# The second FFN pass of a hybrid attention/mLSTM step: its down products as scaled float16 pairs, in groups of 6, 6, 6 and 4 tiles

## The chip, the cores and the metric

The program runs on one core of one Trainium2 chip, in one launch. The metric is the device time of an execution in microseconds (us), compared by the median of several runs. One execution was also recorded by the hardware profiler; all traces and profile lines are of such an execution.

Engines are written as in the profile: PE is TensorE's matmuls, PEld its weight loads, DVE is VectorE, ACT is ScalarE, POOL is GpSimd, SP is SyncE, whose queue issues most loads.

## The reference

One step of a hybrid diffusion backbone in float32: 128 prompt tokens and 1024 latent tokens, model width 1024, one layer. Attention and a bidirectional mLSTM memory stand side by side, then one output projection, then a SwiGLU FFN of width 2816. Only the FFN and what is behind it matter here:

```python
def swiglu(h, w_gu, w_down):
    g, u = jnp.split(h @ w_gu, 2, axis=-1)
    return (jax.nn.silu(g) * u) @ w_down
...
    h2 = rmsnorm(x, norm2_w) * (1 + sc2) + sh2
    x = x + g2 * swiglu(h2, w_gu, w_down)
...
y = rmsnorm(x, final_norm_w)
```

`w_gu` is 1024 x 5632, `w_down` is 2816 x 1024. The 1152 tokens are 9 blocks of 128.

## The kernel before

**Tiling.** The width of the FFN is cut into 22 tiles (NF) of 128. The FFN runs twice over all weights. A first pass does blocks 0 to 2 (the prompt and two latent blocks). The second pass does the other 6 blocks (768 tokens), and the change is in it.

**Precision by pairs.** A value is split into a high part and a remainder ("hi" and "lo"), and a product of two such values is three matmuls: hi·hi, hi·lo and lo·hi. The gate and up products of the second pass use pairs of float16, scaled by powers of two that are found at run time: `six` holds those scales, and `wsum` row sums from which a bound on the weights is made (`tally` in `load_piece`, then `weight_scale` and `power_scale`). The down products use pairs of float32r instead, without a scale.

**The second pass, tile by tile.** `pair6` makes one tile f of the FFN's width for all 768 tokens, in a scheme of 7 products instead of 8 (Strassen's kind). Each product is 12 matmuls of 128x128 by 128x384, so a tile, called a pair from here on, is 84 matmuls. `weights6` loads the two weight halves (512 KB each) and makes the operands `A` of the products: four sums `S` on VectorE, then scaled high halves on ScalarE and low halves on VectorE. Between products, ScalarE copies the first product (`p1`) and takes two Tanh (`tn`), and VectorE does the other sums. At a pair's end `hl` holds the activation of tile f: high half by ScalarE (L1663), low half by VectorE (L1664).

**Down products.** After a group of tiles (`SIX`: 4, 4, 4, 4, 3, 3), `down6` loads that group's rows of `w_down`, two tiles of 512 columns to a piece (512 KB). For each half n of the width and each of 6 blocks, `down_block6` adds three matmuls of 128x128 by 128x512 per tile into one PSUM bank; `hl` is the stationary operand. That is 22 x 12 x 3 = 792 matmuls. `add_gated` (L1205 and L1206, on VectorE) then multiplies the bank by the gate `gs6` and adds it to the tokens' rows: 12 times per group, 72 times in all. The last group goes through `down_last`, which also does the final RMSNorm of a block and writes it out.

**What sets the order.** The program is written once and a scheduler with a simulated timeline orders each engine's instructions; so the down products of a group end up among and behind products of the next pair. Tiles have tags with a fixed number of buffers. There are four raw buffers for weights that come in as float32, and four pieces, each a high and a low half, under four tags of two buffers. A piece is used again in turn. Eight PSUM banks serve the whole pass. SyncE's queue issues loads in its order.

Of the kernel before, what the change touches and what calls it, by code (L numbers as in the profile page):

```python
# [8 lines left out]
F32 = mybir.dt.float32  # L9
F32R = mybir.dt.float32r  # L10
F16 = mybir.dt.float16
# [38 lines left out]
def hybrid_step(ctx: ExitStack, tc: tile.TileContext, I: dict, O: dict):  # L50
# [24 lines left out]
    def emit(gen):  # L75
        for _ in gen:
            pass
# [79 lines left out]
    def load_piece(srcs, shape, raw=None, own=None, tally=None):  # L157

        a, b = shape
        n = a * b  # L160

        def view(t):
            return t[:, :n].rearrange("p (a b) -> p a b", b=b)

        raw = raw_tile() if raw is None else raw
        if not own:
            loaded["n"] = (loaded["n"] + 1) % len(piece_tags)
            tag = piece_tags[loaded["n"]]
# [5 lines left out]
        nc.scalar.copy(hi[:, :n], raw[:, :n])  # L174
        sub(lo[:, :n], raw[:, :n], hi[:, :n].bitcast(F32), "dve")
        if tally is not None:
            jk = ft.tile([P, D], BF16, name=nm("jk"), tag="t2", bufs=nt2[0])
            act(jk[:, :n], hi[:, :n].bitcast(F32), AF.Abs, accum_out=wsum[:, tally : tally + 1])
        return view(hi), view(lo)

    full_view = lambda v: v
# [13 lines left out]
    def power_scale(tp, one, bound, out):  # L195
# [4 lines left out]
        dve.tensor_reduce(out=v[:, 0:1], in_=ps[0:1, 0:P], axis=AX.X, op=ALU.max)  # L200
        powers(v, 1)
# [1326 lines left out]
    def six_scales():  # L1528

        dve.tensor_reduce(out=six[:, 6:7], in_=shift2[:, :, 1], axis=AX.X, op=ALU.max, apply_absolute_value=True)  # L1530
        dve.tensor_reduce(out=six[:, 7:8], in_=scale2[:, :, 1], axis=AX.X, op=ALU.max, apply_absolute_value=True)
        dve.scalar_tensor_tensor(out=six[:, 7:8], in0=six[:, 7:8], scalar=float(D) ** 0.5, in1=six[:, 6:7], op0=ALU.mult, op1=ALU.add)
        yield
        yield from power_scale(fp, ones, six[:, 7:8], six[:, 0:2])
        for t, src in ((0, scale2), (1, shift2)):
            dve.tensor_scalar(out=mods6[:, :, t], in0=src[:, :, 1], scalar1=six[:, 0:1], scalar2=None, op0=ALU.mult)
        yield

    def weight_scale():

        dve.tensor_reduce(out=six[:, 7:8], in_=wsum, axis=AX.X, op=ALU.max)
        emit(power_scale(fp, ones, six[:, 7:8], six[:, 2:4]))
# [71 lines left out]
    def pair6(f, Bt, acts):  # L1614
# [45 lines left out]
        dve.tensor_tensor(out=tn[:, 0], in0=tn[:, 0], in1=a, op=ALU.mult)  # L1660
        hl = new_hl(f)
        flat = tn.rearrange("p a n -> p (a n)")
        act(hl[:, 0], flat, AF.Copy, scale=six[:, 6:7])  # L1663
        dve.scalar_tensor_tensor(out=hl[:, 1], in0=flat, scalar=six[:, 6:7], in1=hl[:, 0].bitcast(F32), op0=ALU.mult, op1=ALU.subtract)  # L1664
        acts.append(hl)
        yield

    late_hl = {}

    def new_hl(f):  # L1670
        if f % 6 < 4:
            return up.tile([P, 2, 2 * CT], F32R, name=nm("hl"), tag="hl", bufs=4)
        if "t" not in late_hl:
            late_hl["t"] = rowp.tile([P, 2, 2, 2 * CT], F32R, name="hl_late", tag="b4")
        return late_hl["t"][:, f % 6 - 4]

    def down_pieces6(f0, nf, n):
        pieces = []
        for j in range(0, nf, 2):
            m = min(2, nf - j)  # L1680
            rows = w_down[(f0 + j) * P : (f0 + j + m) * P, n * 512 : (n + 1) * 512].rearrange("(a p) n -> p a n", p=P)
            pieces.append(load_piece([(full_view, rows)], (m, 512)))
        return pieces

    def down_block6(ps, pieces, acts, i):
        nf = len(acts)
        sl = slice(i * P, (i + 1) * P)
        for k, hl in enumerate(acts):
            wh, wl = pieces[k // 2]
            mm(ps, hl[:, 0, sl], wh[:, k % 2, :], start=(k == 0), stop=False)  # L1690
            mm(ps, hl[:, 0, sl], wl[:, k % 2, :], start=False, stop=False)  # L1691
            mm(ps, hl[:, 1, sl], wh[:, k % 2, :], start=False, stop=(k == nf - 1))  # L1692

    def down6(x1, acts, f0, nf, gs):
        for n in range(2):
# [79 lines left out]
    six = sx.tile([P, 8], F32, name="six")  # L1775
    wsum = sx.tile([P, 2 * NF], F32, name="wsum")
# [77 lines left out]
    for tag, n, bufs in (("p1", CT, 2), ("u2", CT, 2), ("u3", CT, 1), ("c22", CT, 1), ("c21", CT, 1), ("gb", CT, 1), ("tn", 2 * CT, 2), ("hl", 4 * CT, 4)):  # L1854
# [5 lines left out]
    x6 = nxt["x1"] + far["x1"]  # L1860
    gs6 = row_pair(g_d[1, 1])
    done6 = finish(0, cur)
    for f0, nf in SIX:
# [66 lines left out]
```

## Time and profile before

| | |
|---|---|
| Median of 3 runs | 1511.7 us (1509.88 to 1512.18) |
| The profiled execution: its own time, its span | 1510.05 us, 1508.2 us |
| Granted TensorE clock over the span | 0.984 |
| Busy: PE, weight loads, DVE, ACT, POOL | 1419.4, 1059.8, 1129.3, 812.7, 219.5 us |
| First product of the second pass | at 1004.1 us |
| Start of the last pair's last matmul | at 1466.03 us |
| Start of the last matmul of all | at 1488.59 us |

Times in the trace count from the span's start. Busy time of an engine is the sum of its records, and shares are of the span. Matmuls are pipelined, so their records overlap: the time between their starts tells what one costs, not the record's length. Idle time of an engine is put down to what released it last.

### The profile page before, as it was taken

Reading aid. Unit: us, or ns where it says so; the run is one execution under the profiler, and the core shown is the slowest. Engines: PE = TensorE matmul, PEld = TensorE weight load, DVE = VectorE, ACT = ScalarE, POOL = GpSimd, SP = SyncE. Lnnn points to the kernel's source line nnn. Section 1 sums busy time; section 2 is a strip of 40 time slices with the busy share of each in tenths; the row PEclk is TensorE's granted clock in tenths of the full one; section 3 lists DMA queues with packets and bytes.
Section 4 is the critical chain, followed back from the end, with each engine's and each line's share of the span. In section 5 each row is a group of like instructions: output and inputs, shape, how many; then the busy total and the mean of one; then the engine's idle time right before and its main releaser. Section 6 shows DMA issues by size and latency. Waiting matters only on the chain.

```text
span 1508.2 us, 22751 instructions
## 1 busy us (share of the span) xinstructions
PE 1419.4 (94%) x8282; PEld 1059.8 (70%) x8282; DVE 1129.3 (75%) x2280; ACT 812.7 (54%) x1525; POOL 219.5 (15%) x310
## 2 busy tenths in 40 slices
PE   6889999998899789999999989999999999999994
PEld 3635667766677567988998978976767667676763
DVE  4978556775877978658687757899877695977857
ACT  4854476966867645555675854854243240524233
POOL 0112423232224335310100000100000000000000
PEclk9899999999999899999999999999999999999997
DMA  9575224654567855756586744344132130312112
GB/s 369 166 209 192 86 69 78 128 97 74 97 150 161 202 174 143 208 171 190 173 189 161 190 110 153 123 136 163 48 96 72 42 126 15 126 50 77 35 36 84
DMA packets 253029, 194.92 MB, mean 129 GB/s; under 512 B 166702, under 2 KB 207878, under 8 KB 252918
## 3 DMA queue, kind: packets, MB, share of 16 engines
q1 hardware_dynamic: 249918, 187.46, 45.8%
q10 hardware_dynamic: 2872, 5.62, 1.1%
q8 instruction: 65, 1.06, 0.3%
q14 instruction: 46, 0.38, 0.1%
q0 software_dynamic: 128, 0.39, 0.1%
HBM read 141.84 MB, written 13.26 MB: 103 GB/s over the span
## 4 chain that ended last, share of the span: by engine, by line
PE 47%; DVE 6%; ACT 2%; DMA 1%; issue 1%; SPq 0%; DVEq 0%; ACTq 0%
PE mm L1622 5%; PE mm L1623 5%; PE mm L1624 5%; PE mm L1690 4%; PE mm L1691 4%; PE mm L1692 4%; PE mm L1474 3%; PE mm L1476 3%; PE mm L1475 3%; PE mm L1216 2%; PE mm L1217 2%; PE mm L1218 2%; PE S L1128 1%; PE po L1153 1%; DVE A L1609 1%
## 5 line engine op out<-in xcount | busy, mean ns | idle before, releaser
L1623 PE MATMUL mm<-Bt,A 128*128 128x384 f16 x616 | 200.8, 326 | 0.0
L1622 PE MATMUL mm<-Bt,A 128*128 128x384 f16 x616 | 199.3, 326 | 0.3 <-DVE c L1643 0.3
L1624 PE MATMUL mm<-Bt,A 128*128 128x384 f16 x616 | 197.4, 326 | 0.0
L174 ACT CAST whi<-raw 128x1024 fp32r<-128x1024 f32 (+1 forms) x102 | 103.2, 1013 | 123.0 <-DMA raw<-in_w_down_dram 45.4
L145 DVE TENSOR_TENSOR wlo<-raw,whi 128x1024 fp32r<-128x1024 f32 (+1 forms) x102 | 122.1, 1198 | 35.4 <-ACT whi L174 32.2
L1135 DVE SCALAR_TENSOR_TENSOR pl<-pr,st,ph 128x1152 f16<-128x1152 f32 (+1 forms) x72 | 95.1, 1321 | 37.4 <-ACT ph L1134 37.4
L1474 PE MATMUL mm<-aTh,whi 128*128 128x384 f32 x352 | 119.7, 340 | 0.7 <-DVE tn L1493 0.7
L1476 PE MATMUL mm<-aTh,wlo 128*128 128x384 f32 x352 | 119.1, 338 | 0.0
L1475 PE MATMUL mm<-aTl,whi 128*128 128x384 f32 x352 | 118.9, 338 | 0.0
L1131 ACT ACTIVATE pr<-S,st 128x1152 f32<-128x1152 f32 (+1 forms) x72 | 81.5, 1132 | 54.1 <-DVE st L1130 52.7
L1130 DVE TENSOR_REDUCE st<-S 128x1 f32<-128x1152 f32 (+1 forms) x72 | 88.9, 1234 | 23.7 <-PE S L1128 23.5
L526 PE MATMUL wi<-headw,hT 128*128 128x384 f16 x288 | 93.9, 326 | 1.2 <-ACT th L816 1.2
L527 PE MATMUL wi<-headw,hT 128*128 128x384 f16 x288 | 93.9, 326 | 0.0
L528 PE MATMUL wi<-headw,hT 128*128 128x384 f16 x288 | 93.9, 326 | 0.0
L1128 PE MATMUL S<-kst,qT 128*128 128x384 f32 (+1 forms) x400 | 87.6, 348 | 4.0 <-ACT pr L1131 4.0
L1608 ACT ACTIVATE A<-S,six 128x1024 f16<-128x1024 f32 x44 | 49.8, 1145 | 75.8 <-PE mm L1624 54.8
L1134 ACT ACTIVATE ph<-pr,st 128x1152 f16<-128x1152 f32 (+1 forms) x72 | 83.7, 1162 | 12.5 <-ACT pr L1131 4.8
L1622 PEld LDWEIGHTS <-A 128*128 128x128 f16 x616 | 60.2, 98 | 42.5 <-issue 3.3
L1624 PEld LDWEIGHTS <-A 128*128 128x128 f16 x616 | 60.3, 98 | 39.8
L1623 PEld LDWEIGHTS <-A 128*128 128x128 f16 x616 | 60.3, 98 | 39.3 <-issue 0.4
L1205 DVE TENSOR_TENSOR t<-mm,hmr 128x512 f32<-128x512 f32 x84 | 54.5, 683 | 43.3 <-PE mm L1692 32.0
L145 POOL TENSOR_TENSOR hl<-tn,hl 128x384 fp32r<-128x384 f32 x22 | 30.6, 1390 | 319.5 <-ACT hl L1497 265.5
(466 smaller groups left out, 3724.9 us busy)
## 6 DMA issues: line engine op xcount, KB each, us to landing
raw<-in_w_gu_dram SPq DMA_DIRECT2D x88, 512.0 KB, 3.8
raw<-in_w_down_dram SPq DMA_DIRECT2D x40, 512.0 KB, 3.9
a<-in_w_ada_dram SPq DMA_DIRECT2D x24, 512.0 KB, 6.5
iraw<-in_w_in_dram SPq DMA_DIRECT2D x32, 256.0 KB, 3.1
x<-in_x_sample_dram SPq DMA_DIRECT2D x11, 512.0 KB, 5.4
raw<-in_w_out_dram SPq DMA_DIRECT2D x10, 512.0 KB, 4.1
aw<-in_w_ada_dram SPq DMA_DIRECT2D x8, 512.0 KB, 5.2
aw<-in_w_ada_dram SPq DMA_DIRECT2D x16, 256.0 KB, 8.0
```

The lines of the kernel that those rows point to most:

```text
L145: (dve if eng == "dve" else pool).tensor_tensor(out=out, in0=full, in1=hi, op=ALU.subtract)
L174: nc.scalar.copy(hi[:, :n], raw[:, :n])
L526: mm(ps[:, :n], ah, wh[:, k % 2, c0 : c0 + n], start=(k == 0), stop=False)
L527: mm(ps[:, :n], ah, wl[:, k % 2, c0 : c0 + n], start=False, stop=False)
L1128: mm(S[:, n, 0:w], qT[:, h, :], kst[kv][:, t, c0 + n * w : c0 + (n + 1) * w], start=(t == 0), stop=(t == 1))
L1135: dve.scalar_tensor_tensor(out=plv, in0=prv, scalar=st[:, 3:4], in1=phv, op0=ALU.mult, op1=ALU.subtract)
L1474: mm(ps, wh[:, k, :], th[:, k, :], start=(k == 0), stop=False)
L1475: mm(ps, wh[:, k, :], tl[:, k, :], start=False, stop=False)
L1476: mm(ps, wl[:, k, :], th[:, k, :], start=False, stop=(k == KD - 1))
L1622: mm(ps, wh[:, k], bt[:, 0, k], start=first and k == 0, stop=False, skip_group_check=True)
L1623: mm(ps, wh[:, k], bt[:, 1, k], start=False, stop=False, skip_group_check=True)
L1624: mm(ps, wl[:, k], bt[:, 0, k], start=False, stop=k == 3, skip_group_check=True)
```

## The change

The down products of the second pass become pairs of scaled float16.

- `hl` is float16 and scaled by a constant, `DOWN_C` = 2^-46. A third step is new: ScalarE writes `h2`, the high half times 2^11, and the low half is taken against it, itself scaled by 2^11. There are 7 + 4 places for tiles of `hl`, not 4 + 2.
- `half_piece` makes the weight pieces: the high half scaled by `six[:, 8:9]` on ScalarE, the low half on VectorE, and a copy of the high half times 2^-11 on ScalarE, for the product with the low half of `hl`.
- The weights' scale must be known first. `down_tally` loads each of the 22 row tiles of `w_down` (128 x 1024, 512 KB) one time more, into the buffers of the pieces, and sums the absolute values of its rows on ScalarE. These steps are put one by one between the products of pairs 0 to 4 by the code's order. After pair 4 `down_scale` makes the scale (a maximum, a transpose and a product with ones on TensorE, and small operations), and two operations on ScalarE put the inverse scales into the gates `gs6`.
- `SIX` is 6, 6, 6, 4.
- In the first pass the tally of the gate and up weights sums squares in place of absolute values, `power_scale` takes a root by a shift for it, and a bound for the tokens' scale is made with one operation of another form.

```diff
-SIX = [(0, 4), (4, 4), (8, 4), (12, 4), (16, 3), (19, 3)]
+SIX = [(0, 6), (6, 6), (12, 6), (18, 4)]
+DOWN_C = 2.0 ** -46
...
-            act(jk[:, :n], hi[:, :n].bitcast(F32), AF.Abs, accum_out=wsum[:, tally : tally + 1])
+            act(jk[:, :n], hi[:, :n].bitcast(F32), AF.Square, accum_out=wsum[:, tally : tally + 1])
...
+    def down_tally(j):
+
+        loaded["n"] = (loaded["n"] + 1) % len(piece_tags)
+        tag = piece_tags[loaded["n"]]
+        raw = homes.get(tag, wp).tile([P, D], F32, name=nm("whi"), tag=tag, bufs=2)
+        dma(raw, w_down[j * P : (j + 1) * P, :])
+        jk = ft.tile([P, D], BF16, name=nm("jk"), tag="t2", bufs=nt2[0])
+        act(jk, raw, AF.Abs, accum_out=wsum[:, 2 * NF + j : 2 * NF + j + 1])
+
+    def tallies():
+
+        for j in range(NF):
+            down_tally(j)
+            yield
+
+    def down_scale():
+
+        n = NF
+        dve.tensor_reduce(out=six[:, 7:8], in_=wsum[:, 2 * NF : 2 * NF + n], axis=AX.X, op=ALU.max)
+        emit(power_scale(up, ones, six[:, 7:8], six[:, 8:10]))
+        dve.scalar_tensor_tensor(out=six[:, 10:11], in0=six[:, 6:7], scalar=1.0 / DOWN_C, in1=six[:, 9:10], op0=ALU.mult, op1=ALU.mult)
...
-        act(hl[:, 0], flat, AF.Copy, scale=six[:, 6:7])
-        dve.scalar_tensor_tensor(out=hl[:, 1], in0=flat, scalar=six[:, 6:7], in1=hl[:, 0].bitcast(F32), op0=ALU.mult, op1=ALU.subtract)
+        act(hl[:, 0], flat, AF.Copy, scale=DOWN_C)
+        h2 = up.tile([P, 2 * CT], F32, name=nm("h2"), tag="h2", bufs=1)
+        act(h2, hl[:, 0], AF.Copy, scale=2.0 ** 11)
+        dve.scalar_tensor_tensor(out=hl[:, 1], in0=flat, scalar=DOWN_C * 2.0 ** 11, in1=h2, op0=ALU.mult, op1=ALU.subtract)
...
-            pieces.append(load_piece([(full_view, rows)], (m, 512)))
+            pieces.append(half_piece(rows, m))
...
+    def half_piece(rows, m):
+        raw = raw_tile()
+        n = m * 512
+        loaded["n"] = (loaded["n"] + 1) % len(piece_tags)
+        tag = piece_tags[loaded["n"]]
+        at = homes.get(tag, wp)
+        hi, lo = [at.tile([P, 2, 1024], F16, name=nm(t), tag=tag, bufs=2) for t in ("whi", "wlo")]
+        dma(raw[:, :n].rearrange("p (a b) -> p a b", b=512), rows)
+        act(hi[:, 0, :n], raw[:, :n], AF.Copy, scale=six[:, 8:9])
+        dve.scalar_tensor_tensor(out=lo[:, 0, :n], in0=raw[:, :n], scalar=six[:, 8:9], in1=hi[:, 0, :n], op0=ALU.mult, op1=ALU.subtract)
+        act(hi[:, 1, :n], hi[:, 0, :n], AF.Copy, scale=2.0 ** -11)
+        return hi, lo
...
-            mm(ps, hl[:, 1, sl], wh[:, k % 2, :], start=False, stop=(k == nf - 1))
+            mm(ps, hl[:, 1, sl], wh[:, 1, ws], start=False, stop=(k == nf - 1))
...
             for _ in pair6(f, Bt, acts):
                 if f > 0:
                     next(done6, None)
+                next(to_tally, None)
+            if f == 4:
+                for _ in to_tally:
+                    pass
+                down_scale()
+                for g in gs6:
+                    act(g, g, AF.Copy, scale=six[:, 10:11])
```

The scheduler orders the second pass anew; up to SyncE's load of the first weights of the pass nothing moves. At three places the order stands as follows.

SyncE's queue, where the loads of the second pass begin, before (`raw` are weights as they come in: 2217 and 2218 those of pair 0, 2272 and 2273 of pair 2, 2243 and 2244 of pair 1; `fw` and `gx` belong to the first blocks' end):

```order
L1596 DMA raw_2217_11235<-in_w_gu_dram 128x1024
L1596 DMA raw_2218_11237<-in_w_gu_dram 128x1024
L1194 DMA gx_2206_11208<-g_d_81 128x512
L1518 DMA fw_2255_11487<-in_final_norm_w_dram 128x512
L1518 DMA fw_2256_11489<-in_final_norm_w_dram 128x512
L1596 DMA raw_2272_11615<-in_w_gu_dram 128x1024
L1596 DMA raw_2243_11448<-in_w_gu_dram 128x1024
```

and after, where `whi` from `w_down` are the loads of tallies, and 2302 and 2258 are of pairs 2 and 1:

```order
L1622 DMA raw_2217_11237<-in_w_gu_dram 128x1024
L1556 DMA whi_2236_11359<-in_w_down_dram 128x1024
L1556 DMA whi_2248_11431<-in_w_down_dram 128x1024
L1622 DMA raw_2218_11239<-in_w_gu_dram 128x1024
L1556 DMA whi_2239_11377<-in_w_down_dram 128x1024
L1556 DMA whi_2251_11452<-in_w_down_dram 128x1024
L1198 DMA gx_2206_11210<-g_d_81 128x512
L1522 DMA fw_2270_11520<-in_final_norm_w_dram 128x512
L1622 DMA raw_2302_11678<-in_w_gu_dram 128x1024
L1556 DMA whi_2241_11393<-in_w_down_dram 128x1024
L1556 DMA whi_2256_11477<-in_w_down_dram 128x1024
```

Two loads of tallies have moved in front of pair 0's second weights, and more stand ahead of the weights of pairs 1 and 2.

ScalarE, behind the last `A` of pair 1, before (`tn` is a Tanh of pair 0, `A` 2275 to 2277 are operands of pair 2, `p1` copies pair 1's first product):

```order
L1608 ACTIVATE A_2249_11466<-raw_2244_11450,six_6947 128x512
L1647 ACTIVATE tn_2239_11410<-mm_2231_11338,six_6947 128x384
L1608 ACTIVATE A_2275_11624<-raw_2272_11615,six_6947 128x2x512
L1631 COPY p1_2254_11485<-mm_2250_11469 128x384
L1608 ACTIVATE A_2276_11627<-S_2274_11619,six_6947 128x2x512
```

and after, from the same operand of pair 1 to the same copy and on to the operands of pair 2 (`jk` are the tallies):

```order
L1634 ACTIVATE A_2264_11499<-raw_2259_11483,six_6947 128x512
L1558 ACTIVATE jk_2281_11552,wsum_6948<-whi_2280_11550 128x1024
L1673 ACTIVATE tn_2247_11429<-mm_2231_11341,six_6947 128x384
L1558 ACTIVATE jk_2284_11573,wsum_6948<-whi_2283_11571 128x1024
L1634 ACTIVATE A_2305_11687<-raw_2302_11678,six_6947 128x2x512
L1558 ACTIVATE jk_2286_11592,wsum_6948<-whi_2285_11590 128x1024
L1558 ACTIVATE jk_2290_11612,wsum_6948<-whi_2289_11610 128x1024
L1678 ACTIVATE tn_2247_11429<-gb_2250_11447,six_6947 128x384
L1558 ACTIVATE jk_2293_11630,wsum_6948<-whi_2292_11628 128x1024
L1657 COPY p1_2269_11518<-mm_2265_11502 128x384
L1558 ACTIVATE jk_2296_11651,wsum_6948<-whi_2295_11649 128x1024
L1558 ACTIVATE jk_2301_11676,wsum_6948<-whi_2300_11674 128x1024
```

Between the operand and the copy stand five tallies that were not there, and both Tanh of pair 0 in place of one.

TensorE, at the first down products of the pass, before (row by row, `hl` 2242 and 2271 are tiles 0 and 1; the first row is the end of a product of pair 3, and no weight loads have rows of their own for float32r):

```order
L1624 MATMUL mm_2298_11767<-Bt_9893,A_2294_11755 128x384
L1690 MATMUL mm_2316_11889<-whi_2311_11878,hl_2242_11445 128x512
L1691 MATMUL mm_2316_11889<-wlo_2312_11879,hl_2242_11445 128x512
L1692 MATMUL mm_2316_11889<-whi_2311_11878,hl_2242_11445 128x512
L1690 MATMUL mm_2316_11889<-whi_2311_11878,hl_2271_11612 128x512
L1691 MATMUL mm_2316_11889<-wlo_2312_11879,hl_2271_11612 128x512
```

and after (the first row is of pair 5):

```order
L1650 MATMUL mm_2388_12145<-Bt_9893,A_2384_12133 128x384
L1732 LDWEIGHTS hl_2254_11472
L1732 MATMUL mm_2410_12278<-whi_2402_12258,hl_2254_11472 128x512
L1733 LDWEIGHTS hl_2254_11472
L1733 MATMUL mm_2410_12278<-wlo_2403_12259,hl_2254_11472 128x512
L1732 LDWEIGHTS hl_2254_11472
L1732 MATMUL mm_2412_12300<-whi_2402_12258,hl_2254_11472 128x512
```

The first down products have moved from pair 3 to pair 5; the longest runs of them in one piece are 114 before and 198 after, and the run at the end is 97 before and 131 after. The 792 float16 products each have a weight load as a row. The last 131 of them, not the last 97, come behind all pair products.

More of the change, by code (lines that the diff above doesn't have):

```diff
@@ L193, in powers, with power_scale @@
         dve.tensor_scalar(out=v[:, 3:4], in0=v[:, 1:2], scalar1=2.0 ** -12, scalar2=None, op0=ALU.mult)
-    def power_scale(tp, one, bound, out):
+    def power_scale(tp, one, bound, out, squares=False):
         ps = bank()
@@ L200, in power_scale @@
         dve.tensor_reduce(out=v[:, 0:1], in_=ps[0:1, 0:P], axis=AX.X, op=ALU.max)
+        if squares:
+            dve.tensor_scalar(out=v[:, 1:2].bitcast(I32), in0=v[:, 0:1].bitcast(I32), scalar1=1, scalar2=None, op0=ALU.logical_shift_right)
+            dve.tensor_scalar(out=v[:, 0:1].bitcast(I32), in0=v[:, 1:2].bitcast(I32), scalar1=1, scalar2=0x1FC00000, op0=ALU.mult, op1=ALU.add)
         powers(v, 1)
@@ L1531, in six_scales @@
         dve.tensor_reduce(out=six[:, 7:8], in_=scale2[:, :, 1], axis=AX.X, op=ALU.max, apply_absolute_value=True)
-        dve.scalar_tensor_tensor(out=six[:, 7:8], in0=six[:, 7:8], scalar=float(D) ** 0.5, in1=six[:, 6:7], op0=ALU.mult, op1=ALU.add)
+        dve.tensor_scalar(out=six[:, 7:8], in0=six[:, 7:8], scalar1=six[:, 6:7], scalar2=float(D) ** 0.5, op0=ALU.add, op1=ALU.mult)
         yield
@@ L1539, in weight_scale @@
     def weight_scale():
-        dve.tensor_reduce(out=six[:, 7:8], in_=wsum, axis=AX.X, op=ALU.max)
-        emit(power_scale(fp, ones, six[:, 7:8], six[:, 2:4]))
+        dve.tensor_reduce(out=six[:, 7:8], in_=wsum[:, 0 : 2 * NF], axis=AX.X, op=ALU.max)
+        emit(power_scale(fp, ones, six[:, 7:8], six[:, 2:4], squares=True))
         dve.tensor_tensor(out=six[:, 4:5], in0=six[:, 1:2], in1=six[:, 3:4], op=ALU.mult)
@@ L1689, in down_block6 @@
             wh, wl = pieces[k // 2]
-            mm(ps, hl[:, 0, sl], wh[:, k % 2, :], start=(k == 0), stop=False)
-            mm(ps, hl[:, 0, sl], wl[:, k % 2, :], start=False, stop=False)
-            mm(ps, hl[:, 1, sl], wh[:, k % 2, :], start=False, stop=(k == nf - 1))
+            ws = slice(k % 2 * 512, k % 2 * 512 + 512)
+            mm(ps, hl[:, 0, sl], wh[:, 0, ws], start=(k == 0), stop=False)
+            mm(ps, hl[:, 0, sl], wl[:, 0, ws], start=False, stop=False)
+            mm(ps, hl[:, 1, sl], wh[:, 1, ws], start=False, stop=(k == nf - 1))
     def down6(x1, acts, f0, nf, gs):
@@ L1774, in hybrid_step @@
     sx = ctx.enter_context(tc.tile_pool(name="sx", bufs=1, reuse_waits="tile"))
-    six = sx.tile([P, 8], F32, name="six")
-    wsum = sx.tile([P, 2 * NF], F32, name="wsum")
+    six = sx.tile([P, 12], F32, name="six")
+    wsum = sx.tile([P, 4 * NF], F32, name="wsum")
     mods6 = sx.tile([P, KD, 2], F32, name="mods6")
@@ L1862, in hybrid_step @@
     done6 = finish(0, cur)
+    to_tally = tallies()
     for f0, nf in SIX:
```

10 lines of the change are left out of this document (5 added, 5 removed).

## The prediction

> **What bounds the kernel now.** I read the page first, its engine line, chain and groups; then the stretches of the second pass, TensorE's own timeline in it, and the end on VectorE.
>
> ```profile
> span 1508.2 us, 22751 instructions
> PE 1419.4 (94%) x8282; PEld 1059.8 (70%) x8282; DVE 1129.3 (75%) x2280; ACT 812.7 (54%) x1525; POOL 219.5 (15%) x310
> PE 47%; DVE 6%; ACT 2%; DMA 1%; issue 1%; SPq 0%; DVEq 0%; ACTq 0%
> ```
>
> TensorE is busy 94% and has the largest part of the chain. Whether that holds where the change is made, the stretches say (columns: us, then busy us and instructions of PE, weight loads, DVE, ACT, POOL, the granted clock, the DMA share, GB/s).
>
> ```profile
> 1004.10:1466.40 462.30, 462.01 (x2545) 310.42 (x2545) 363.89 (x551) 160.50 (x201) 0.00 (x0) 1.00 0.24 77
> 1004.10:1061.60 57.50, 57.50 (x346) 35.57 (x346) 56.34 (x92) 30.57 (x40) 0.00 (x0) 1.00 0.49 160
> 1466.40:1489.20 22.80, 22.58 (x97) 17.84 (x95) 15.22 (x36) 7.53 (x17) 0.00 (x0) 1.00 0.06 23
> 1489.20:1508.20 19.00, 0.00 (x0) 0.00 (x0) 14.41 (x43) 8.46 (x22) 0.00 (x0) 0.60 0.36 138
> ```
>
> From the first product of the pass (1004.1) to the end of the last pair's products (1466.4, called T0 below) TensorE has 0.3 us free of 462.3, at clock 1.00. What other engines save there is worth nothing by itself; a shorter matmul is worth its full time, and any wait put into it costs its full time. Behind T0 stand 97 down products, and behind 1489.2 TensorE does nothing: that end belongs to other engines. The spacing of matmuls is read from starts in TensorE's timeline, since records overlap:
>
> ```profile
> 1057.42 0.34 PE L1622 MATMUL mm<-Bt,A 128*128 128x384 f16 x1
> ...
> 1059.22 0.33 PE L1624 MATMUL mm<-Bt,A 128*128 128x384 f16 x1
> ...
> 1059.61 0.39 PE L1690 MATMUL mm<-whi,hl 128*128 128x512 f32 x1
> ...
> 1062.17 0.40 PE L1692 MATMUL mm<-whi,hl 128*128 128x512 f32 x1
> ...
> 1488.59 0.40 PE L1692 MATMUL mm<-whi,hl 128*128 128x512 f32 x1
> ```
>
> Pair products: 11 intervals in 1.80 us, 0.163 (0.1625 over longer stretches). Down products in float32r: 11 intervals in 2.56, 0.2327. As a check, 1848 x 0.1625 + (792 - 97) x 0.2325 = 300.3 + 161.6 = 461.9 against the 462.3 of the stretch: the count explains it all.
>
> **The change, part by part.**
>
> *Float16 down products.* The trace has a float16 matmul of this very shape (128x128 by 128x512, each with a weight load of its own), in the input projection:
>
> ```profile
> 108.25 0.27 PE L124 MATMUL mm<-ident,vm 128*1 128x128 f32 x1
> 108.36 0.38 PE L526 MATMUL wi<-ipair,hT 128*128 128x512 f16 x1
> ...
> 111.38 0.38 PE L528 MATMUL wi<-ipair,hT 128*128 128x512 f16 x1
> ```
>
> From the second row on, 14 intervals in 3.02 us: 0.216. There are 792 products before and after, so the format gives 792 x 0.0165 = 13.1 us at most. The last group now has four tiles, and by TensorE's order 131 of its products come behind the last pair, not 97. So ahead of T0: 300.3 + 661 x 0.216 = 443.1 against 462.3, **-19.1 us**, of which 34 x 0.2325 = 7.9 is work that goes behind T0. [...]
>
> *The tail.* What decides it is when VectorE finishes:
>
> ```profile
> 1469.89 1.02 DVE L1664 SCALAR_TENSOR_TENSOR hl<-tn,six,hl 128x768 fp32r<-128x768 f32 x1 [1.00 <-ACT hl L1663]
> 1476.18 0.69 DVE L1205 TENSOR_TENSOR t<-mm,hmr 128x512 f32<-128x512 f32 x1 [5.28 <-PE mm L1692]
> ...
> 1482.25 0.67 DVE L1205 TENSOR_TENSOR t<-mm,hmr 128x512 f32<-128x512 f32 x1
> 1486.51 0.68 DVE L1205 TENSOR_TENSOR t<-mm,hmr 128x512 f32<-128x512 f32 x1
> 1490.76 0.67 DVE L1205 TENSOR_TENSOR t<-mm,hmr 128x512 f32<-128x512 f32 x1
> ```
>
> VectorE waits for the first closed bank (1476.18, T0 + 9.8), then goes at 4.26 us a block until the end, T0 + 42. Now the first bank closes after 46 products, 46 x 0.216 = 9.9, as before after 42 x 0.2325 = 9.8. The last bank closes at 131 x 0.216 = T0 + 28.3 (before 22.6). VectorE takes its last bank at about T0 + 32.9 (start of block 1 at 15.9, four more of 4.26 each). So the 34 extra products are covered with 4.6 us over, and the tail stays at 42. If that cover were gone, 34 x 0.216 = 7.3 us would come back.
>
> *Wait for the last act.* Its new third step, the copy h2 (128x768, 0.93 by L1663 below), puts the low half, which ended at 1470.91 (T0 + 4.5), at about T0 + 5.5. TensorE's order has 36 products behind the last pair before the first that reads it: T0 + 7.8. Nothing.
>
> *The tallies.* 22 loads and 22 Abs sums with accumulation, all in the first five pairs. The rows that price them:
>
> ```profile
> L178 ACT ACTIVATE jk<-whi x44: 1041/1052/1082, 635.4 to 974.2; 128x1024 bf16<-128x1024 f32 x44
> L1608 ACT ACTIVATE A<-raw,six 128x1024 f16<-128x1024 f32 x21 | 23.9, 1138 | 2.0 <-DMA raw<-in_w_gu_dram 2.0
> L174 ACT CAST whi<-raw 128x1024 fp32r<-128x1024 f32 x20 | 20.9, 1048 | 30.8 <-DMA raw<-in_w_down_dram 26.9 <-PE mm L1691 3.8
> L1663 ACT ACTIVATE hl<-tn,six 128x768 fp32r<-128x768 f32 x15 | 14.0, 933 | 16.7 <-DVE tn L1654 14.1 <-DVE tn L1660 2.5
> L1652 ACT ACTIVATE tn<-gb,six 128x384 f32<-128x384 f32 x22 | 13.4, 608 | 11.4 <-DVE gb L1651 11.4
> ACT p L1631 <- PE mm L1624: 100.4, 7, 25.1
> ACT A L1608 <- PE mm L1624: 87.5, 32, 5.6
> raw<-in_w_gu_dram SPq DMA_DIRECT2D x88, 512.0 KB, 3.8
> 1026.00:1029.00 3.00, 3.00 (x20) 1.79 (x19) 3.00 (x5) 2.15 (x4) 0.00 (x0) 1.00 1.03 418
> ```
>
> In the 57.5 us from 1004.1 ScalarE is busy 30.6. Four weight casts leave that stretch (-4.2), 22 sums come (22 x 1.05 = 23.1) and two copies h2 (1.9): 51.4 of 57.5. It fits, but ScalarE works in order, and before each instruction for which TensorE waits there now stand tallies. The narrowest place is the copy p1 of pair 1: TensorE adds its fifth product into the same bank, so the copy has three products' time, 36 x 0.1625 = 5.85 us. Ahead of it, behind the last A of that pair, stand five tallies, one A and two Tanh: 5.25 + 1.14 + 1.18 = 7.6. Some of that starts before the first product has closed; walking on with these durations, and with loads at the rate of the peak row, I get waits of about 1.35 us there, 0.7 for pair 2's first operands, and 0.8 and 0.6 in pairs 3 and 4. **+3.5 us**. Bounds: 0, if ScalarE runs ahead (TensorE has nothing to gain), and 22 x (1.05 + 0.19 for reading the sum) = 27.3, if every tally stands on TensorE's path. Near the low end, since ScalarE in this pass waits for TensorE far more than the reverse (the two waits rows).
>
> Bytes: 22 x 0.52 = 11.5 MB, 28 us at the peak of 418 GB/s. The stretch of 57.5 us has a DMA share of 0.49, so about half is free, and by SyncE's order the first tallies are issued while the first pass still runs: it fits too. Two tallies pass the second half of pair 0's weights on that queue; their buffers are free when it is issued, so they cost it 2 x 1.25 = 2.5 us of transfer, ahead of the S sums, which have that slack.
>
> *The scale.* A transpose and a product with ones on TensorE, 0.1 us each by the L124 row above (next start 0.11 later): **+0.3** with their switches. The chain of small VectorE operations behind them must end before the first weight piece is converted, a pair later. The gates scaled twice on ScalarE, once: in pair 5, hidden.
>
> *Weight pieces.* The nearest rows:
>
> ```profile
> L145 DVE TENSOR_TENSOR wlo<-raw,whi 128x1024 fp32r<-128x1024 f32 x26 | 31.9, 1227 | 2.0 <-ACT whi L174 1.4
> L1609 DVE SCALAR_TENSOR_TENSOR A<-raw,six,A 128x1024 f16<-128x1024 f32 x22 | 28.1, 1277 | 10.0 <-ACT A L1608 10.0
> L1205 DVE TENSOR_TENSOR t<-mm,hmr 128x512 f32<-128x512 f32 x72 | 46.3, 682 | 32.2 <-PE mm L1692 32.0
> ```
>
> Three operations per piece, not two: ScalarE gains one (1.05 by L174), and VectorE's subtraction goes from 1.23 to 1.28 at most. Groups of six need six pieces in four slots, so the fifth and sixth wait for the last block of the first half; TensorE's order has 25 products (5.4 us) between, against 1.05 + 1.28. Hidden.
>
> *Fewer groups.* 24 of 72 gated additions fall away (two operations of 0.68 each, L1205 and the sum behind it): -32.8 us on VectorE, off the path, so nothing. In the first pass the Square costs what the Abs did.
>
> Sum: -19.1 + 3.5 + 0.3 = -15.3. The profiled execution took 1510.05 (span 1508.2 and 1.85 around it), the median is 1.65 above it. So the span goes to 1492.9, the profiled execution to 1494.7, the median to **1496.4**.
>
> **The rivals.**
>
> *The tallies starve the first pairs (slower).* Each tally waits for its load at the head of ScalarE's order. If loads landed one by one at 3.8 us, 22 + 12 of them for six pairs would take 129 us against 6 x 84 x 0.1625 = 82: +47, net +28, 1540. It turns the sign when the waits pass 18.8 us, that is when a load costs on average (82 + 18.8) / 34 = 3.0 us. Against it: the peak row moves one in 1.25 us, and several are in flight. For it: eight tally buffers free themselves only through ScalarE, and idle TensorE also loses clock here:
>
> ```profile
> 500.00:550.00 50.00, 41.03 (x240) 29.15 (x238) 39.74 (x110) 25.13 (x66) 19.53 (x20) 0.90 0.70 185
> ```
>
> 41 us busy of 50 goes with a clock of 0.90. [...] A milder form, with waits of 10 to 18 us, ends at 1503 to 1511.
>
> *No wait at all.* ScalarE's free time absorbs the tallies: -18.8, 1492.9.
>
> *The format gives nothing.* If these products keep 0.2325, since operands and banks are laid out differently from the input projection's, only the 34 moved ones are gained: -7.9 + 3.8 = -4.1, 1507.6. Against it is the 0.216 of the same shape.
>
> [...]
>
> **How the numbers follow.** The forecast (waits of 1 to 9 us, 1493.5 to 1502) 0.62; no wait 0.11; nothing from the format 0.05; the mild starvation 0.09; the full one 0.11; the 0.131 0.02. The 0.2% (3 us) that a measurement here can tell from no change splits the mild case: half of it is faster, half the same. So faster 0.62 + 0.11 + 0.05 + 0.02 + 0.04 = 0.84, same 0.05, slower 0.11. The range goes from 1491 (no wait, less the 1.8 us by which the lowest of the runs shown lies under their median) to 1507, where waits reach 14 us.
>
> **What the next profile would show.** Spacing of the down products 0.216, weight loads shorter than before, T0 about 15 us earlier, with no idle TensorE behind pair 5. Waits of TensorE between 1004 and 1072 of 3 to 4 us in sum, released by ScalarE (copy p1 or A), none above 2. The end at T0 + 42, VectorE's chain still at 4.26 a block. I'm wrong if waits for tally loads show on ScalarE and TensorE's clock falls there, if VectorE in the tail waits for banks after its first, or if gaps open at the groups' starts on pieces.

## The result and the profile after

| | before | changed |
|---|---|---|
| Median, first comparison (4 runs each) | 1511.87 us | 1501.15 us (1499.85 to 1502.16) |
| Ratio to before, 95% interval | | 0.9931 [0.9914, 0.9949] |
| Median, second comparison, other chip (11 and 6 runs) | 1512.25 us | 1500.61 us (1495.82 to 1502.38) |
| Ratio, 95% interval | | 0.9923 [0.9911, 0.9935] |
| Profiled execution: its time, its span | 1510.05, 1508.2 us | 1501.71, 1499.9 us |

The change makes the kernel faster by 10.7 to 11.6 us. The forecast was 1496.4, a gain of 15.3; the measured medians lie 4.2 to 4.8 us above it. First the page of the changed kernel:

```profile
span 1499.9 us, 22798 instructions
PE 1412.5 (94%) x8285; PEld 992.8 (66%) x8285; DVE 1101.7 (73%) x2240; ACT 872.4 (58%) x1613; POOL 219.7 (15%) x310
PE 48%; DVE 4%; DMA 2%; ACT 2%; issue 1%; SPq 0%; ACTq 0%; DVEq 0%
```

TensorE still has the largest part of the chain. The stretches that answer to those of before (columns as there) are: the second pass up to the last pair's end, its first 61.7 us, the products behind it, and the end.

```profile
1009.60:1457.60 448.00, 444.85 (x2514) 245.49 (x2514) 335.80 (x506) 218.21 (x286) 0.00 (x0) 1.00 0.30 100
1009.60:1071.30 61.70, 58.69 (x355) 34.31 (x355) 51.69 (x89) 51.23 (x83) 0.00 (x0) 1.00 0.71 264
1457.60:1485.90 28.30, 28.30 (x132) 12.69 (x130) 20.28 (x51) 11.55 (x27) 0.00 (x0) 1.00 0.10 38
1485.90:1499.90 14.00, 0.13 (x1) 0.00 (x0) 9.35 (x28) 5.29 (x14) 0.00 (x0) 0.60 0.39 150
```

The pass takes 448.0 us where it took 462.3. The two rows are cut at slightly different points behind the last pair product; from the start of the first pair product to the start of the last it is 447.8 and 461.9, so 14.1 less. In its first pairs TensorE is now free for 3.0 of 61.7 us and ScalarE is busy for 51.2. But the pass starts at 1009.6, not at 1004.1: 5.5 us are lost ahead of it. The pass with its waits came near the forecast; the miss lies mostly where the forecast put no change.

TensorE's timeline in the middle of the pass shows the down products (L1732 to L1734):

```profile
1093.83 0.38 PE L1733 MATMUL mm<-wlo,hl 128*128 128x512 f16 x1
...
1095.99 0.38 PE L1732 MATMUL mm<-whi,hl 128*128 128x512 f16 x1
```

10 intervals in 2.16 us: 0.216 each, as in the input projection. The tail, on VectorE:

```profile
1467.72 0.69 DVE L1209 TENSOR_TENSOR t<-mm,hmr 128x512 f32<-128x512 f32 x1 [4.70 <-PE mm L1734]
...
1473.78 0.67 DVE L1209 TENSOR_TENSOR t<-mm,hmr 128x512 f32<-128x512 f32 x1
...
1478.03 0.67 DVE L1209 TENSOR_TENSOR t<-mm,hmr 128x512 f32<-128x512 f32 x1
...
1482.29 0.67 DVE L1209 TENSOR_TENSOR t<-mm,hmr 128x512 f32<-128x512 f32 x1
```

Counted from one spacing (0.16) behind the start of the last pair product, it starts after 10.1 us (before 10.0), goes on at 4.25 to 4.26 us a block, and ends after 42.3 us (before 42.0), with 34 more products under it.

What TensorE waited for from 980 on, in the changed kernel (engine, line, what it waited for, us in sum, times, longest):

```profile
PE mm L1220 <- DVE t L1209: 2.8, 1, 2.8
PE mm L1650 <- DVE A L1635: 1.8, 2, 1.4
PE mm L1648 <- DVE u L1667: 0.5, 1, 0.5
PE mm L1648 <- ACT A L1634: 0.5, 1, 0.5
```

The last three are in the second pass; they are only the longer ones, and by the starts of its matmuls TensorE loses 4.1 us in the first five pairs. The first is in the last down products of the first pass, where before had this:

```profile
PE mm L1216 <- DVE t L1205: 1.4, 1, 1.4
```

And behind that longer wait TensorE's clock falls. Stretches of 5 us, first of the changed kernel, then of before (PEclk is the third figure from the right):

```profile
995.00:1000.00 5.00, 2.96 (x7) 2.34 (x8) 4.39 (x11) 0.00 (x0) 0.00 (x0) 0.73 0.93 342
```

```profile
995.00:1000.00 5.00, 5.00 (x23) 4.11 (x22) 5.00 (x9) 1.10 (x1) 0.00 (x0) 1.00 0.28 102
```

Matmuls that started 0.23 us apart before start 0.43 apart there:

```profile
993.42 0.85 PE L1222 MATMUL mm<-whi,hl 128*128 128x512 f32 x3
997.04 0.64 PE L1220 MATMUL mm<-whi,hl 128*128 128x512 f32 x1 [2.77 <-DVE t L1209]
997.47 0.63 PE L1221 MATMUL mm<-wlo,hl 128*128 128x512 f32 x1
```

**Where that wait comes from.** At the end of the first pass `weight_scale` makes the scale of the gate and up weights. With squares it has to take a root, which is two more small operations on VectorE, one after the other, each with a large operation put between. VectorE's timeline in the changed kernel (L203 and L204 are the root; L191 to L194 stood there before too, as L190 to L193):

```profile
992.00 0.13 DVE L203 TENSOR_SCALAR pv<-pv 1x1 int32<-1x1 int32 x1
992.07 0.67 DVE L146 TENSOR_TENSOR wlo<-raw,whi 128x512 fp32r<-128x512 f32 x1
992.67 0.13 DVE L204 TENSOR_SCALAR pv<-pv 1x1 int32<-1x1 int32 x1
992.73 1.20 DVE L146 TENSOR_TENSOR Bt<-T,Bt 128x1024 f16<-128x1024 f32 x1
993.86 0.13 DVE L191 TENSOR_SCALAR pv<-pv 1x1 f32<-1x1 f32 x1
...
995.06 0.67 DVE L1209 TENSOR_TENSOR t<-mm,gx 128x512 f32<-128x512 f32 x1
...
995.72 1.27 DVE L1209 TENSOR_TENSOR t<-mm,gl 128x512 f32<-128x512 f32 x2
```

The scheduler put the product with ones (L208) behind a block of 15 down products instead of ahead of it, and gave that block the bank that VectorE reads third, not first; presumably because it saw the chain end later. In TensorE's order, changed kernel:

```
L1222 MATMUL mm_2200<-whi_2195,hl_2186 128x512
L1220 MATMUL mm_2225<-whi_2208,hl_2127 128x512     (waits for the third t, L1209)
... 14 more of this block
L208  MATMUL mm_2203<-pv_2202,ones_6950 128x2
```

and before:

```
L1218 MATMUL mm_2200<-whi_2195,hl_2186 128x512
L204  MATMUL mm_2203<-pv_2202,ones_6950 128x2
L1216 MATMUL mm_2216<-whi_2208,hl_2127 128x512     (waits for the first t, L1205)
```

That is a reading so far; the experiments test it.

### The profile page after: what moved, and what is told of

The parts are those of the page before. It is cut to its first block, busy times and chain, and to the rows that moved or that the text cites. A ratio compares the mean times of both kernels' runs of the same rounds, so it can differ in the third digit from the quotient of the medians.

```text
span 1499.9 us, 22798 instructions
## 1 busy us (share of the span) xinstructions
PE 1412.5 (94%) x8285; PEld 992.8 (66%) x8285; DVE 1101.7 (73%) x2240; ACT 872.4 (58%) x1613; POOL 219.7 (15%) x310
## 4 chain that ended last, share of the span: by engine, by line
PE 48%; DVE 4%; DMA 2%; ACT 2%; issue 1%; SPq 0%; ACTq 0%; DVEq 0%
PE mm L1650 5%; PE mm L1648 5%; PE mm L1649 5%; PE mm L1478 3%; PE mm L1479 3%; PE mm L1480 3%; PE mm L1732 3%; PE mm L1733 3%; PE mm L1734 3%; PE mm L1220 2%; PE mm L1221 2%; PE mm L1222 2%; PE S L1132 1%; DMA raw<-in_w_down_dram 1%; PE po L1156 1%
## 5 line engine op out<-in xcount | busy, mean ns | idle before, releaser
L175 ACT CAST whi<-raw 128x1024 fp32r<-128x1024 f32 (+1 forms) x78 | 79.7, 1024 | 75.9 <-PE mm L1221 30.8
L146 DVE TENSOR_TENSOR wlo<-raw,whi 128x1024 fp32r<-128x1024 f32 (+1 forms) x78 | 95.0, 1219 | 33.5 <-ACT whi L175 31.0
L1650 PEld LDWEIGHTS <-A 128*128 128x128 f16 x616 | 60.3, 98 | 42.3 <-DVE A L1635 2.6
L1132 PEld LDWEIGHTS S<-kst,qT 128*128 128x128 f32 x400 | 69.5, 189 | 7.7 <-ACT pr L1135 5.4
L1209 DVE TENSOR_TENSOR t<-mm,hmr 128x512 f32<-128x512 f32 x60 | 40.5, 685 | 40.1 <-PE mm L1734 28.7
```

The lines of the kernel that those rows point to most:

```text
L146: (dve if eng == "dve" else pool).tensor_tensor(out=out, in0=full, in1=hi, op=ALU.subtract)
L1132: mm(S[:, n, 0:w], qT[:, h, :], kst[kv][:, t, c0 + n * w : c0 + (n + 1) * w], start=(t == 0), stop=(t == 1))
L1650: mm(ps, wl[:, k], bt[:, 0, k], start=False, stop=k == 3, skip_group_check=True)
```

## The experiments

### The start of the second pass: e4, e1, e5

**e4**: the kernel before with the first pass's edits only.

```diff
-            act(jk[:, :n], hi[:, :n].bitcast(F32), AF.Abs, accum_out=wsum[:, tally : tally + 1])
+            act(jk[:, :n], hi[:, :n].bitcast(F32), AF.Square, accum_out=wsum[:, tally : tally + 1])
...
+        if squares:
+            dve.tensor_scalar(out=v[:, 1:2].bitcast(I32), in0=v[:, 0:1].bitcast(I32), scalar1=1, scalar2=None, op0=ALU.logical_shift_right)
+            dve.tensor_scalar(out=v[:, 0:1].bitcast(I32), in0=v[:, 1:2].bitcast(I32), scalar1=1, scalar2=0x1FC00000, op0=ALU.mult, op1=ALU.add)
...
-        emit(power_scale(fp, ones, six[:, 7:8], six[:, 2:4]))
+        emit(power_scale(fp, ones, six[:, 7:8], six[:, 2:4], squares=True))
```

> The kernel before with nothing but the first pass's edits (squares, the root, the one-operation bound). Theory: the product with ones moves here too, so it gets slower by the wait and the slow clock, 3.3 to 5.6 us: 1515 to 1517.5 us. Rival (tallies at fault): the same as before, 1512.

Measured: 1515.41 us (12 runs) against 1511.86 (23 runs), ratio 1.0015 [0.9999, 1.0031]: the median is 3.6 us longer and within what was expected, though the interval just reaches 1. The trace has the wait and the clock, here at half:

```profile
996.01 0.79 PE L1219 MATMUL mm<-whi,hl 128*128 128x512 f32 x1 [2.77 <-DVE t L1208]
```

```profile
996.00:1001.00 5.00, 4.99 (x12) 3.93 (x13) 4.37 (x9) 0.00 (x0) 0.00 (x0) 0.50 0.36 98
```

There is no tally of `w_down` in this kernel, so the tallies don't make this wait. The run has the Square, the root and the new form of the bound together. The next one keeps the form of the bound; the Square and the root were not tried apart.

**e1**: the changed kernel with the sums of absolute values again (`AF.Abs`, no `squares=True`, and `DOWN_C = 2.0 ** -38`).

> The changed kernel with the first pass's tally of the gate and up weights put back to absolute values and without the root (DOWN_C becomes 2^-38, since that scale is 2^4 smaller). Theory: the two operations of the root made the scheduler put the product with ones behind a block of 15 down products, whose bank comes free late (a wait of 2.8 us, then some 4 us at half clock); here the product with ones stands first again, the second pass starts 5.6 us earlier, and the time is 1495.5 us (1494 to 1497). Rival: the tallies' loads, two of which now stand ahead of pair 0's second weights, hold up the start of the second pass; they are unchanged here, so 1500 to 1502.

Measured: 1500.58 us (1497.69 to 1503.44; 6 runs), ratio 0.9921 [0.9902, 0.9939]. The expected 1495.5 did not come: by the runs it can't be told from the changed kernel. The time is the one that the rival gave, but the trace doesn't bear the rival out, and says why the gain is less than expected. The product with ones stands ahead again, and the pass starts at 1004.1 as before, with a short wait and the clock at 1.00:

```profile
993.57 0.51 PE L1220 MATMUL mm<-whi,hl 128*128 128x512 f32 x1 [1.28 <-DVE t L1209]
```

But the pass itself takes 449.4 us, 1.5 more than in the changed kernel, since the other product with ones, that of the down weights' scale, now waits:

```profile
PE mm L208 <- DVE pv L194: 2.0, 1, 2.0
```

So 1.8 to 3.3 us are gained ahead of the pass, against the changed kernel's two traces below, and 1.5 are lost in it.

**e5**: the changed kernel with `weight_scale()` called one step earlier (`if i == 2:`).

> The changed kernel with the scale of the gate and up weights begun one step earlier in the last down products of the first pass (i == 2 in place of 3). Squares, root and tallies stay, and the product with ones still stands behind a block of 15 down products; but that block's bank is now the one that VectorE frees first, not third. Theory (the wait is for the bank, and the slow clock follows from its length): a wait of 1.3 to 1.7 us, no slow matmuls, the second pass 3.3 us earlier against the transpose of the bound, and 3 us less than the changed kernel's time in this call. Rival (the late scale itself holds up the first operands): start as late as in the changed kernel, and its time.

Measured: 1500.49 us (1498.21 to 1500.81; 5 runs) against 1500.61 for the changed kernel in the same comparison: the 3 us expected did not come; the time is the rival's. The wait, though, is shorter, at the upper edge of what was expected, and no matmul is slow:

```profile
PE mm L1220 <- DVE t L1209: 1.7, 1, 1.7
```

Against the transpose of the bound the pass starts no earlier (20.7 us behind it, 20.5 and 19.0 in the changed kernel's two traces), since the transpose itself has moved ahead with the call; the table counts from a product instead.

The three and the others of this study together, from the start of the last product ahead of the wait to the first pair:

| product with ones | kernel | wait, us | matmuls 0.43 apart | to the first pair, us |
|---|---|---|---|---|
| ahead of the block | before, e1, e8 | 1.3 to 1.4 | 0 | 12.5 |
| behind, first bank | e5 | 1.7 | 0 | 13.2 |
| behind, third bank | changed (second comparison), e6 | 2.8 | 0 | 14.3, 14.2 |
| behind, third bank | changed (first), e2 | 2.8 | 8, 7 | 15.8 |
| behind, third bank | e3, e4 | 2.8 | 13 | 17.0, 16.9 |

So the order (the small product behind the block, and that block in the third bank) costs 1.8 us by the wait, and up to 2.7 more where the clock falls behind it, which it did in four of six traces with the same wait. What an average execution loses there isn't known, since only profiled ones show it.

**The changed kernel again**, for comparison on one chip:

> The changed kernel once more, for a comparison on one chip: 1501 us (1499 to 1503), with a wait of 2.8 us and some slow matmuls at the start of the second pass.

1500.61 us. Its profiled execution happened to be the fastest of six (1495.82): no slow matmuls, and the transpose of the bound, up to which the two executions run one program, came at 984.6 where the first one has 989.1. Such a spread of 4.5 us within the first pass, from one execution to another of the same kernel, is as large as what is being looked for; that is why I compare stretches within a trace. The granted clock over the span was 0.988 in this execution and 0.980 in the first; whether the spread comes from that is not shown.

One stretch leaves the first pass's spread out and can be read in every trace: from the first of the last 90 down products of the first pass, the same matmul of TensorE's order in all of them, to the end of the span.

| kernel | from that product to the end, us |
|---|---|
| before; e4 | 526.8; 531.0 |
| e3; e8 | 525.5; 518.0 |
| changed, its two traces | 516.4, 515.1 |
| e1; e2; e5; e6 | 514.6; 515.2; 514.1; 513.4 |
| e7, its two traces; e9 | 510.9, 510.1; 512.7 |

By this the change gains 10.5 to 11.8 us, as the medians say. The gains of e1 and e5 over the changed kernel, 0.5 to 2.3 us, show here, but they are hardly more than the 1.3 us between its own two traces, and too little for medians of five or six runs to show.

### The tallies: e2, e6, e7

**e2**: no tallies; the scale is 2^13, set by `memset`.

> The changed kernel without the second reading of w_down: no loads, no sums, the scale is a constant (2^13). The squares and the root of the first pass stay. Theory: only TensorE's waits in pairs 0 to 4 go (4.1 us) and the two small products (0.3): 1496.7 us (1495.5 to 1498), and the wait at the start of the second pass, with the slow clock behind it, is still there. Rival: the tallies make the late start as well; then 5.6 more, 1491.

1502.53 us (6 runs), ratio 0.9928 [0.9910, 0.9946]: no gain, and neither of the two times expected. As expected the wait and the slow clock ahead of the pass are still there. But the pass takes 446.8 us, only 1.1 less than with tallies. The waits of the first pairs went, and others came:

```profile
PE mm L1645 <- DVE u L1664: 2.1, 2, 1.9
```

VectorE's timeline at that place:

```profile
1078.29 1.28 DVE L1719 SCALAR_TENSOR_TENSOR wlo<-raw,six,whi 128x1024 f16<-128x1024 f32 x1 [1.21 <-ACT whi L1718]
1079.49 1.28 DVE L1632 SCALAR_TENSOR_TENSOR A<-S,six,A 128x1024 f16<-128x1024 f32 x1
...
1081.25 0.55 DVE L1664 TENSOR_TENSOR u<-mm,u 128x384 f32<-128x384 f32 x1
```

The subtraction of a new weight piece stands at the head of VectorE's order and waits 1.21 us for ScalarE, and the sum `u`, for which TensorE waits, stands behind it.

**e6**: each tally's sum over 128 of 1024 columns, loads whole (`jk[:, 0:128], raw[:, 0:128]`).

> The changed kernel with each tally's sum over 128 of the 1024 columns; the 22 loads stay whole. (The scale is then that of an eighth of the weights.) Theory (ScalarE's order: the sums stand ahead of operands): TensorE's waits in pairs 0 to 4 fall from 4.1 to 1.5 us or less, since a sum takes about 0.2 in place of 1.05. Rival (the loads: they share the DMA engines with the weights of the next pairs, which land 2 to 3 us later): 3 to 4 us remain.

TensorE's waits in the first five pairs fall from 4.1 to 1.9 us (matmul starts 0.85 and 1.34 us apart at two places instead of 0.16), between the two theories and nearer to the first. (The 0.2 us for a sum over 128 columns is an estimate; in the changed kernel's trace ScalarE's next instruction starts 0.95 us behind the start of a sum over 1024 columns, L1558, and 0.54 behind one over 512, L1770.) By this about half of the wait is the sums' time on ScalarE, and the rest goes with the loads or the order. In the changed kernel there is one place where ScalarE waited long for weights (longest before: 2.0):

```profile
1016.21 1.15 ACT L1634 ACTIVATE A<-raw,six 128x1024 f16<-128x1024 f32 x1 [3.88 <-DMA raw<-in_w_gu_dram]
```

The copy p1 behind it is late, and TensorE loses 0.3 us. But in e6 the same wait is 4.3 us and TensorE loses less than 0.1 there. So what the loads cost by themselves is not shown. The time is 1499.39 us (1493.52 to 1505.0) against 1500.61; that tells nothing.

**e7**: the first pass sums its own 24 pieces of `w_down`, and there is no second reading.

```diff
-            pieces.append(load_piece([(full_view, rows)], (m, 512)))
+            pieces.append(load_piece([(full_view, rows)], (m, 512), tally=2 * NF + downs[0]))
+            downs[0] += 1
...
-    to_tally = tallies()
+    to_scale = down_scale()
...
-                next(to_tally, None)
-            if f == 4:
-                for _ in to_tally:
-                    pass
-                down_scale()
+            if f == 2:
+                next(to_scale)
+            if f == 3:
+                emit(to_scale)
```

(`down_scale` yields between its two steps, and `weight_scale` is called at `i == 2`.)

> The changed kernel without the second reading of w_down: the first pass's 24 weight pieces of w_down are summed where they are loaded anyway, the scale is made in two steps behind pairs 2 and 3, and the scale of the gate and up weights begins one step earlier as in the run above. Theory: the start of the second pass comes 3.3 us earlier, the tallies' waits of 4.1 go, of which 3 come back as waits behind VectorE, as without tallies; ScalarE has room in the first pass: 1496 us (1494 to 1499). Rival: the 24 sums (24 x 1.24 = 30 us) hold up TensorE in the first pass; 1500 or more.

> The kernel with the tallies in the first pass once more: 1496 us (1494.5 to 1498.5), pass of 446.9 and tail of 42.2 us. If the first result was chance, 1500.5 as the changed kernel.

1496.23 us (1494.68 to 1503.03), ratio 0.9899 [0.9882, 0.9916], beside the changed kernel's 1500.61; the second time 1498.77 (1496.31 to 1500.97), ratio 0.9907 [0.9892, 0.9923], just above the range expected. It is the fastest kernel of this study, 13 to 16 us below before and 2 to 4 below the changed one (the second time measured on another chip), where the intervals of the ratios overlap. The pass took 446.9 and 446.1 us, 1 to 2 less than the changed kernel's. In both traces TensorE's wait ahead of the pass has gone, but for this:

```profile
PE mm L1220 <- DVE six L209: 0.3, 1, 0.3
```

The last 90 down products take 21.8 us to the first pair, where the changed kernel takes 26.1 and 24.6 (before 22.7). On the other hand these 90 begin at 990.4 and 989.1 us (e9: 989.8), later than in any trace without the sums (979.0 to 986.8). So the sums may take some of the gain back in the first pass, as the rival had it; both profiled executions were the slowest of their six, so this stays open.

### The tail: e3, e8, e9

**e3**: the changed kernel with groups of 6, 6, 7, 3.

> The changed kernel with groups of 6, 6, 7 and 3 tiles: 93 down products behind the last pair, not 131. Theory: the tail goes at VectorE's pace either way, so 38 products of 0.216 us come back ahead of it: +8.2 us, 1509.3 (1508 to 1511). Rival: the tail's length follows TensorE's products, which end 8.2 us earlier in it: 1501, no change.

1510.09 us (12 runs), ratio 0.9981 [0.9967, 0.9995]: as expected by the first theory. The pass is 456.0 us against 448.0, and the tail 42.2:

```profile
1468.80:1489.00 20.20, 20.20 (x95) 9.02 (x92) 12.25 (x27) 7.37 (x16) 0.00 (x0) 1.00 0.00 0
1489.00:1511.00 22.00, 0.06 (x1) 0.00 (x0) 17.37 (x52) 9.49 (x25) 0.00 (x0) 0.60 0.37 143
```

TensorE is done 8 us earlier in the tail, and the end does not move.

**e8**: the kernel before, float32r, with a last group of four.

```diff
-SIX = [(0, 4), (4, 4), (8, 4), (12, 4), (16, 3), (19, 3)]
+SIX = [(0, 4), (4, 4), (8, 4), (12, 3), (15, 3), (18, 4)]
```

> The kernel before, float32r all through, with its groups in another order: 4, 4, 4, 3, 3 and 4 tiles. 133 down products come behind the last pair, not 97. Theory (the tail goes at VectorE's pace and has room for 133 x 0.2325 = 30.9 us of products, where VectorE takes its last bank at 32.9): the pass up to the last pair is 36 x 0.2325 = 8.4 us shorter, the tail 42.0 as before: 1503.7 us (1502.5 to 1505.5). So some 8 us of the change's gain need no float16. Rival (the tail grows by what is put into it): 1512, no change.

1504.1 us (6 runs), ratio 0.9941 [0.9922, 0.9961]. The pass is 453.3 us where 453.7 was expected, and the tail 42.0:

```profile
1009.50:1462.80 453.30, 453.30 (x2509) 303.44 (x2509) 363.85 (x550) 160.50 (x201) 0.00 (x0) 1.00 0.24 79
1462.80:1493.90 31.10, 31.10 (x134) 24.76 (x132) 23.31 (x59) 11.81 (x29) 0.00 (x0) 1.00 0.13 51
```

So a change of the groups alone gives 8.1 us, with no float16, no scale and no second reading. In the traces float16 takes the pass from there to 448.0, 5.3 us less, tallies and all, and the edits of the first pass that came with it lose 1.8 to 3.3 again at the start (up to 4.5 in e3 and e4). By the runs e8 and the changed kernel can't be told apart: the intervals of their ratios overlap. And e3, which has all of float16 but only 93 products behind the last pair (97 before), is 1.8 us below before. So most of the gain of 10.7 to 11.6 us comes from the products that moved, and little of it from the format, whose faster matmuls pay for its own waits first.

**e9**: e7 with one multiplication per block of the tail on GpSimd.

```diff
-                    dve.tensor_tensor(out=v, in0=v, in1=fw[:, 0:512], op=ALU.mult)
+                    pool.tensor_tensor(out=v, in0=v, in1=fw[:, 0:512], op=ALU.mult)
```

> The same with the tail's multiplication of a block's first half by the norm's gain on GpSimd, not on VectorE (once per block). Theory (VectorE's chain sets the tail): 0.6 us less per block for five or six blocks, so the tail goes from 42.2 to 39 us, and the time to 1493 (1491.5 to 1495.5); TensorE's last bank at T0 + 28.3 still comes before VectorE wants it at 29.9. Rival (GpSimd's operation, at 1.4 us for 384 columns some 1.9 us for 512, holds up the block's sums or VectorE): tail of 42 or more.

1500.02 us, ratio 0.9919 [0.9901, 0.9938]; the tail is 43.2 us, not 39. GpSimd's timeline, then VectorE's:

```profile
1480.81 1.27 POOL L1776 TENSOR_TENSOR x<-x,fw 128x512 f32<-128x512 f32 x1 [2.99 <-ACT jk L1773]
```

```profile
1481.28 0.82 DVE L1754 TENSOR_TENSOR lq<-lq 128x1 f32<-128x1 f32 x1
1482.02 0.68 DVE L1210 TENSOR_TENSOR x<-x,t 128x512 f32<-128x512 f32 x1
```

A VectorE operation on one column, 0.15 us elsewhere, takes 0.82 here and ends at 1482.10, when GpSimd's ends (1480.81 + 1.27 = 1482.08). In the first block it is a sum that takes longer, 1.78 us in place of 0.68:

```profile
1471.69 1.78 DVE L1210 TENSOR_TENSOR x<-x,t 128x512 f32<-128x512 f32 x1
```

VectorE's chain goes at 4.32 us a block; in the changed kernel, with no work on GpSimd there, it goes at 4.25 to 4.26. Moving work to the idle engine lengthened the chain.

## Why the prediction was right or wrong, point by point

- **TensorE bounds the pass; a matmul is worth its spacing.** Right. The spacing is 0.216, and the pass without its waits is 443.2 us (448.0 less 4.8) against a worked-out 443.1. (The forecast's 462.3 less 443.1 is 19.2, not 19.1; it changes nothing.)
- **34 products go under VectorE's tail.** Right: tail 42.3 against 42.0 (e3 and e8 show it both ways).
- **Waits in the first pairs, +3.5.** 4.1 in the trace (seven places of 0.13 to 1.56 us). The places were not all those foretold: the copy p1 was not the narrowest, but the operand `A` of pair 2 (1.4 us by VectorE's half, behind ScalarE's). Taking them away would not gain that much, as e2 shows.
- **The scale, +0.3.** 0.3. Waits in later groups, which I put at nothing, made another 0.3.
- **In the first pass the Square costs what the Abs did: nothing.** This is the step that failed. The Square's own time is the same (1.052 us, as the Abs had), but the root behind it lengthened a chain of single-element operations, and the scheduler moved the product with ones and changed the bank that the next block waits for. I had counted the instructions of that edit, and not looked at where the scheduler put the last products of the first pass. It cost 1.8 us by the wait and, in the profiled execution, 1.5 more by the clock: 15.8 us to the first pair, not 12.5.
- **The sum.** In the profiled execution: -14.1 in the pass (forecast -15.3), +3.3 ahead of it, +0.3 in the tail, and 2.2 by which the first pass came late at the transpose of the bound. That last is within what executions of one kernel differ by (4.5 us between two of the changed kernel). Together -8.3, the difference of the spans. Without that last term it is -10.5, and in the second trace, where the clock did not fall, -11.8; the medians' 10.7 and 11.6 lie between. So of the forecast's 15.3 the traces miss 1.2 to 1.4 in the pass, 0.3 in the tail and 1.8 to 3.3 ahead of the pass. The last pair product started 8.6 us earlier, not about 15, by what was lost ahead of the pass and in the first pass.
- **The rivals.** The tallies did not starve the pass: no wait there was above 1.6 us, and the clock stayed at 1.00 within it. The clock did fall, to 0.73 over 5 us, behind a wait of 2.8 us at a place that no rival named. The chances have a 0.131 as well: no run shows such a spacing, and the float16 down products went 0.216 us apart.

## What to carry to other kernels

Where a scheduler orders the work, an edit that costs nothing by its instructions still has to be followed in the order, above all a longer chain of tiny operations in front of a product. In the changed kernel the product with ones had its operand at 997.71 us (end of L194) and started at 1002.27, behind the block that stood ahead of it. Before a new number format is built for its faster matmuls, look for products that can go under a tail which another engine sets: here that alone gave 8 us, and the format little more. And a wait that is taken away on one engine may come back behind the order of the next (in e2 those of the first pairs went, and the pass became 1.1 us shorter, not 4.1), so it should be priced by an experiment and not by its length.

## What the runs showed of the hardware

- Ahead of the second pass a wait of TensorE of 2.8 us was followed in four traces of six by matmuls 0.43 us apart in place of 0.23, 7 to 13 of them. The clock over 990 to 1015 us was 0.93 in two of the four (changed kernel's first, e2) and 0.86 in the others (e3, e4), with 0.50 over 5 us in e4. In the other two (changed kernel's second, e6) no such matmuls followed, and the clock stayed at 1.00 around the wait in the changed kernel's. Nor did they behind waits of 1.3 to 1.7 us at this place, in four traces. What decides it after 2.8 us is not shown.
- In each of the six blocks of e9's tail one VectorE operation took longer while GpSimd's multiplication (1.26 to 1.30 us) ran: the sum L1210 1.78 and 1.70 us in the first two blocks, in place of 0.68, and the one-column product L1754 0.81 to 0.82 in the other four, in place of 0.15. The excess is 0.66 to 1.1 us. The four of L1754 ended within 0.03 us of GpSimd's end. Not every operation was longer: L1209 took 0.68 and L1775 0.15 beside the third multiplication. Why is not shown.
